# A hybrid layer on one core: k's pairs ahead of q's, constants beside values, staging rows moved, buffers resized

## The chip, the core and the metric

The kernel runs on one core of a Trainium2 chip. TensorE multiplies matrices into PSUM; VectorE, ScalarE and GpSimd work on tiles in SBUF; SyncE (SP) issues the transfers, which sixteen DMA engines carry out. Each engine takes its instructions in the order in which the program holds them, and waits at an instruction until what it needs is there. The metric is the device time of one execution in microseconds; a kernel's time is the median of its runs.

## The reference

One step of a layer over 1088 tokens (1024 of a new stream, 64 of a running one, which also sees 512 cached keys). Cut to what matters here:

```python
xn = _rmsnorm(x, p['norm_mix_w'])
z, xbc, dt_raw, q, k, v, gate_ssm, gate_att = jnp.split(xn @ p['w_in'], ...)
...
q = _partial_rope(_rmsnorm(q.reshape(b, t, 16, 64), p['q_norm_w']), q_pos)
k = _partial_rope(_rmsnorm(k.reshape(b, t, 16, 64), p['k_norm_w']), q_pos)
lam = (jnp.exp(jnp.sum(lambda_q1 * lambda_k1)) - jnp.exp(jnp.sum(lambda_q2 * lambda_k2)) + lambda_init)
o = _diff_attention(q, k_all, v_all, q_pos, k_pos, lam)      # softmax 1 - lam * softmax 2, times v
o = _rmsnorm(o, p['subln_w']) * (1.0 - lambda_init)
mix = sigmoid(gate_ssm) * (y_ssm @ w_branch_ssm) + sigmoid(gate_att) * (o @ w_branch_attn)
x = x + mix @ w_out
x = x + ConvFFN(RMSNorm(x))
```

y_ssm comes from a causal convolution of xbc, a scan over chunks of 64 tokens and a gate of z. k and v are outputs too; q is not.

## The kernel before

All activations lie transposed: 128 channels on the partitions, tokens along the row. A product of float32 is made of three matmuls of rounded parts (hi x hi, lo x hi, hi x lo), so every operand exists as a pair hi and lo: a cast on ScalarE (L355) makes hi, a subtraction on VectorE (L356) makes lo.

The stages stand in this order in the program. **Norm and values.** The input is normed into xn. values(f) (L275) makes a quarter of v from two 512 KB blocks of weights; weights() (L137) loads a block, casts it (L149) and subtracts (L150), with a scheduler's priority `ahead`, which moves these three ahead of other work on their engines. values(0) and values(1) also give dt; steps() (L305) makes the scan's step sizes from it (TensorE L327 to L340). differences() (L367) makes sums of quarters of xn for the next stage, with rows in the pool tt, and stores one of them in t_sc. values(2) and values(3) follow.

**Pairs.** q and k are made by a Strassen-Winograd scheme, two feature blocks at a time: a pair is seven products of blocks, seven() (L563), whose matmuls are L575. Eight pairs run in the order q0, q2, q4, q6, k0, k2, k4, k6. left_blocks() (L426) loads a pair's weights and makes the seven left operands; the next pair's are made during a pair. Each finished row of q or k is squared (L486), and kept raw in r_q or r_k in DRAM (L478).

**finish().** When the four pairs of q (or k) are done, Heads.finish() (L504) sums the squares by four matmuls (L509), makes the reciprocal root (Ln L217, Exp L218, Square L219 on ScalarE) and then runs sixteen rows of 128 channels by 544 tokens: load the raw row (L514), multiply (L516, L518), for k store it as an output (L520), split into hi and lo (L355, L356), store both in q_st or k_st (L524). The tag `fr` of the pool `mid` holds the raw rows, two of them. q's finish runs a row at a time between the products of k's pairs; before it, cached() splits the cached keys in the same manner. k's finish has no pairs left to lie under.

**Filler and attention.** stream() (L689) yields the gate, z and convolution projections in chunks of 24 matmuls (project(), L160; matmuls L156 to L158), each with an evacuation: Tanh for a gate (L641), Tanh (L650) and a multiply (L651) for z. Their rows are staged in the pool st. fill(n) puts n chunks into the program. After k's finish come twelve chunks (FIRST), which the scheduler interleaves with it, then six PSUM banks are released, `mid` is released, `st` is released and made again on the right side of SBUF, and attention runs for eight heads: head_tiles() (L718) loads q, k and v of a head (L722), scores are L764 and L765, and 1.74 chunks of filler go to each unit. Ahead of head 0 stand the constants: wsub (L846), and lam and nlam (L849 to L854). After attention comes the scan with 1.5 chunks for each of its steps, then the branches (attention's o_sc into m_sc and the first half of y_sc into n_sc, as filler under the scan's last steps; the second half of y_sc, whose rows are loaded by L178 and to which g_sc, n_sc and m_sc are brought by L188, after it), the output projection and the FFN.

SP's queue is in order: a store that waits for its row holds all loads behind it.

Of the kernel before, what the change touches and what calls it, by code (L numbers as in the profile page):

```python
# [9 lines left out]
F32 = mybir.dt.float32  # L10
R32 = mybir.dt.float32r
AF = mybir.ActivationFunctionType
ALU = mybir.AluOpType
# [4 lines left out]
P = 128  # L18
# [38 lines left out]
LAST = 200  # L57
ATT_STEPS = 1.74
FIRST = 12
LEFT = dict(fa=8, fs=2)  # L60
MID = dict(fu=4, pr=4, cc=4, ss=4, fr=2)
MIDW = 544
HALF = T // 2
SCAN_STEPS = 1.5
# [17 lines left out]
def hybrid_layer(ctx: ExitStack, tc: tile.TileContext, xT, prm, cst, rope, wvd, win, wbs, wba, wout, wup, wdn,  # L82
# [27 lines left out]
    ident, ones, tri, blk = (con[:, i * P : (i + 1) * P] for i in range(4))  # L110
    eps_t = cp.tile([P, 1], F32, name="eps_t")
    V.memset(eps_t, EPS)

    def col(o):
        return par[:, o : o + 1]
# [16 lines left out]
    xn = [xn_pool.tile([P, KT, T], R32, name=f"xn_{u}") for u in ("hi", "lo")]  # L132
    parts = [[t[:, :, c : c + w] for t in xn] for c, w in WIDE]

    extra, turn, ahead, quick = None, 0, AHEAD_IN, QUICK

    def weights(block, k, m, pool=None):  # L137
        nonlocal turn
        if pool is None:
            turn = (turn + 1) % 3  # L140
        p, b = (pool, 1) if pool is not None else (extra, 1) if extra is not None and turn == 0 else (wp, 2)
        top = WMAX if p is wp else WDT
        w = p.tile([P, top], F32, name="w_f", tag="w_f", bufs=b)
        hi = p.tile([P, top], R32, name="w_hi", tag="w_hi", bufs=b)
        lo = p.tile([P, top], R32, name="w_lo", tag="w_lo", bufs=b)
        w, hi, lo = (t[:, : k * m].rearrange("p (k m) -> p k m", k=k) for t in (w, hi, lo))
        with tc.high_priority(ahead):
            load(out=w, in_=block.rearrange("p (k m) -> p k m", k=k))
            S.copy(hi, w)  # L149
            V.tensor_tensor(out=lo, in0=w, in1=hi, op=ALU.subtract)  # L150
        return hi, lo
# [57 lines left out]
    def run(gen):  # L209
        for _ in gen:  # L210
            pass
# [92 lines left out]
    with tc.tile_pool(name="qk", bufs=1) as qk:  # L304
        def steps():  # L305
            small = lambda n: qk.tile([P, 9, 32], F32, name=n, tag=n)
            da, e, t, t2 = (small(n) for n in ("da", "de", "dt", "dt2"))
            u = dtw
            act(e, u, AF.Abs)
            act(e, e, AF.Exp, scale=-1.0)  # L310
            V.tensor_scalar_add(t, e, 2.0)
            V.reciprocal(t, t)
            V.tensor_tensor(out=t, in0=t, in1=e, op=ALU.mult)
            V.tensor_tensor(out=t2, in0=t, in1=t, op=ALU.mult)
            V.tensor_scalar(e, t2, 1.0 / 17, None, ALU.mult)
            for n in (15, 13, 11, 9, 7, 5, 3):
                V.scalar_tensor_tensor(e, e, 1.0 / n, t2, ALU.add, ALU.mult)
            V.scalar_tensor_tensor(e, e, 1.0, t, ALU.add, ALU.mult)
            V.tensor_scalar_max(u, u, 0.0)
            V.scalar_tensor_tensor(dt_tok, e, 2.0, u, ALU.mult, ALU.add)  # L320
            an = qk.tile([P, 32], F32, name="an")
            act(an, par[:, O_AL : O_AL + 32], AF.Exp)
            V.scalar_tensor_tensor(da, dt_tok, -1.0, an.unsqueeze(1).to_broadcast([P, 9, 32]), ALU.mult, ALU.mult)
            V.memset(da[TS:, 8, :], 0.0)
            flat = lambda x: x.rearrange("p a b -> p (a b)")
            pa = stat(288)
            PE.matmul(pa, tri, flat(da), start=True, stop=True)  # L327
# [4 lines left out]
            V.tensor_tensor(out=flat(dtw), in0=pl, in1=flat(nacum), op=ALU.add)  # L332
            act(dtw, dtw, AF.Exp)
            V.tensor_tensor(out=dtw, in0=dtw, in1=dt_tok, op=ALU.mult)
            af = qk.tile([P, T], F32, name="af")[:32]
            for c, w in WIDE:
                pf = stat(512)
                for i in range(c // P, -(-(c + w) // P)):
                    n = min(P, T - i * P)
                    PE.matmul(pf[:32, i * P - c : i * P - c + n], da[:n, i], tri[:n, :n], start=True, stop=True)  # L340
                V.tensor_copy(af[:, c : c + w], pf[:32, :w])
            load(out=a_sc, in_=af)

        steps()
        load(out=d_sc, in_=dts.rearrange("p a b c -> p (a b c)"))
    dp.release()

# [6 lines left out]
    def split(hi, lo, src):  # L354
        S.copy(hi, src)  # L355
        V.tensor_tensor(out=lo, in0=src, in1=hi, op=ALU.subtract)  # L356
# [47 lines left out]
            differences(s, j)  # L404
    for u in range(2):
        load(out=b_sc[P * u : P * (u + 1), :].rearrange("p (a t) -> p a t", a=4), in_=xn[u][:, :4, HALF:].bitcast(F32))
    for f in (2, 3):
        run(values(f))
    tt.release()
    s1.close()  # L410
    st.release()
    extra.release()
# [13 lines left out]
    def left_blocks(b0, b1):  # L426

        def row(tag, name, dt=F32):
            return lp.tile([P, 512], dt, name=name, tag=tag, bufs=LEFT[tag])

        a = []
        for b in (b0, b1):
            w = wp.tile([P, WMAX], F32, name="w_f", tag="w_f", bufs=2)
            load(out=w, in_=b)
            a += [w[:, :512], w[:, 512:]]
        q11, q12, q21, q22 = a
        s1, s2 = (row("fs", n) for n in ("ws1", "ws2"))
# [11 lines left out]
        G.tensor_tensor(out=q21, in0=q11, in1=q21, op=ALU.subtract)  # L449
        yield own(q21)  # L450
        t = [wp.tile([P, WMAX], R32, name=n, tag=n, bufs=2) for n in ("w_hi", "w_lo")]
        for i, src in enumerate((s1, q22)):
            hi, lo = (x[:, 512 * i : 512 * i + 512] for x in t)
            split(hi, lo, src)
            yield hi, lo
        G.tensor_tensor(out=s2, in0=q12, in1=s2, op=ALU.subtract)
        hi, lo = (wp.tile([P, WMAX], R32, name=n, tag=n, bufs=2)[:, :512] for n in ("w_hi", "w_lo"))
        split(hi, lo, s2)
        yield hi, lo

    psb = ExitStack()
    more = psb.enter_context(tc.tile_pool(name="psb", bufs=6, space=PSUM)), 6
# [149 lines left out]
    heads = {n: Heads(n) for n in "qk"}  # L612
    both = [(p, s) for p in range(7) for s in range(2)]
    begin = [(p, s) for p in (0, 2, 1, 3, 5, 4, 6) for s in range(2)]
    order = [(n, f, f + 1) for n in "qk" for f in range(0, KT, 2)]
    left, finishing = list(blocks_of(*order[0])), cached()
    for n, (kind, f, g) in enumerate(order):
        coming = blocks_of(*order[n + 1]) if n + 1 < len(order) else iter(())
# [8 lines left out]
            if n + 1 == len(order) and (p, s) == (4, 1):  # L627
                fourth(b_sc)
        left = nxt + list(coming)
        if (kind, f) == ("q", 6):  # L630
            finishing = chain(finishing, heads["q"].finish())
    run(finishing)
    lp.release()
    tu.release()
# [69 lines left out]
            spare -= 1  # L704


    run(heads["k"].finish())
    fill(FIRST)
    psb.close()
    more = None, 0  # L710
    mid.release()
    st.release()
    st = tc.alloc_tile_pool(name="st", bufs=1, side="right")
    cv_pool = tc.alloc_tile_pool(name="cv", bufs=1, side="right")

    with (tc.tile_pool(name="ak", bufs=1) as ak, tc.tile_pool(name="at", bufs=1) as at,
          tc.tile_pool(name="psc", bufs=1, space=PSUM) as psc, tc.tile_pool(name="psa", bufs=1, space=PSUM) as pa):
        def head_tiles(h):  # L718
            def fetch(name, n, b, parts):
# [120 lines left out]
                    load(out=o_sc[D * u + P * h : D * u + P * (h + 1), b0 * P : b0 * P + w], in_=t.bitcast(F32))  # L840

        tiles = head_tiles(0)
        lam = at.tile([P, 4], F32, name="lam")
        lt = at.tile([P, 512], F32, name="lt", tag="a_t", bufs=AT)[:, :64]
        wsub = at.tile([P, P], F32, name="wsub")
        V.tensor_scalar_mul(wsub, par[:, O_SUB : O_SUB + P], 1.0 - LAMBDA_INIT)  # L846
        for i in range(2):
            a = O_LAM + 128 * i
            V.tensor_tensor(out=lt, in0=par[:, a : a + 64], in1=par[:, a + 64 : a + 128], op=ALU.mult)  # L849
            V.reduce_sum(lam[:, i : i + 1], lt, axis=AX.X)  # L850
            act(lam[:, i : i + 1], lam[:, i : i + 1], AF.Exp)
        nlam = at.tile([P, 1], F32, name="nlam")
        V.tensor_tensor(out=nlam, in0=lam[:, 1:2], in1=lam[:, 0:1], op=ALU.subtract)
        V.tensor_scalar_add(nlam, nlam, -LAMBDA_INIT)  # L854

        late = []
        for h in range(8):
            if h:
# [18 lines left out]
            late = [lambda h=h, o=o_t, q=ssq, s=s0: head_out(h, o, q, s)]  # L877
        late[0]()


    with (tc.tile_pool(name="sin", bufs=1) as sin, tc.tile_pool(name="sp", bufs=1) as sp,
          tc.tile_pool(name="psi", bufs=1, space=PSUM) as psi, tc.tile_pool(name="pss", bufs=1, space=PSUM) as pss):
# [133 lines left out]

        def branch_tiles():
            nonlocal bs
            cv_pool.release()
            st.release()  # L1020
# [558 lines left out]
```

## Time and profile before

| | us |
|---|---|
| median of 3 runs | 2549.25 (2539.55 to 2556.42) |
| the profiled execution, its own time | 2546.22 |
| its span, first to last instruction | 2544.4 |
| TensorE busy | 2433.2 |
| VectorE busy | 1678.5 |
| ScalarE busy | 1206.7 |
| GpSimd busy | 804.0 |
| granted TensorE clock, mean | 0.984 |

The span is the time between the first and the last instruction in the profile; the execution's own time is a little longer. A row of the list of waits reads: engine, operation and line that waited, the engine, tile and line that released it, the total, the number of times, the longest. A row of the timeline reads: start, duration, engine, line, operation, tile written <- tiles read, shape, and in brackets the idle time of the engine just before it with its releaser.

### The profile page before, as it was taken

To read this page: it belongs to the slowest core of one execution; us is meant where nothing else is said; L and a number is where in the kernel's file an instruction comes from. 1 tells how busy PE (TensorE), PEld (TensorE's weight loads), DVE (VectorE), ACT (ScalarE), POOL (GpSimd) and SP (SyncE) were. 2 spreads that over 40 slices of the span, in tenths; PEclk is the share of its full clock that TensorE was granted. 3 is DMA by queue.
4 is the path that set the end of the run, shared out by engine and by line. 5 is a ranking of instruction groups with operands and counts; after the bars stand their busy time and mean duration, and the time that the engine had idled before them with its cause. 6 is when DMAs were issued, how large, how long until landed. Compare 5 with 4: busy or idle time off the path is not lost. (4 is left out here: it accounts for less than half of the span.)

```text
span 2544.4 us, 45910 instructions
## 1 busy us (share of the span) xinstructions
PE 2433.2 (96%) x17154; PEld 2351.0 (92%) x17154; DVE 1678.5 (66%) x2885; ACT 1206.7 (47%) x2616; POOL 804.0 (32%) x784
## 2 busy tenths in 40 slices
PE   8999985999999999999899999899999999999999
PEld 7999985999999999999798889899999999999999
DVE  7666843775588758645676675564677777777765
ACT  6234442564466646536665564324544343344541
POOL 3235320000011001003443332002466766665445
PEclk9999987999999999999999999999999999999999
DMA  5254789445435543436689763656223444348865
GB/s 176 97 190 171 242 293 307 129 128 166 136 104 152 166 124 112 122 105 206 195 258 304 213 205 116 224 157 214 85 94 126 135 130 137 128 164 247 217 158 169
DMA packets 293776, 432.74 MB, mean 170 GB/s; under 512 B 34576, under 2 KB 210320, under 8 KB 293552
## 3 DMA queue, kind: packets, MB, share of 16 engines
q1 hardware_dynamic: 288944, 420.89, 52.1%
q0 software_dynamic: 4608, 8.91, 2.3%
q8 instruction: 135, 2.21, 0.4%
q14 instruction: 89, 0.73, 0.1%
HBM read 282.18 MB, written 147.52 MB: 169 GB/s over the span
## 5 line engine op out<-in xcount | busy, mean ns | idle before, releaser
L156 PE MATMUL mm<-xn_hi,w_hi 128*128 128x384 f32 (+1 forms) x1632 | 549.3, 337 | 36.7 <-DVE zr L651 26.7
L158 PE MATMUL mm<-xn_hi,w_lo 128*128 128x384 f32 (+1 forms) x1632 | 541.1, 332 | 0.0
L157 PE MATMUL mm<-xn_lo,w_hi 128*128 128x384 f32 (+1 forms) x1632 | 540.9, 331 | 0.0
L156 PEld LDWEIGHTS mm<-xn_hi,w_hi 128*128 128x128 f32 x1632 | 309.4, 190 | 45.9 <-DVE zr L651 27.0
L157 PEld LDWEIGHTS mm<-xn_lo,w_hi 128*128 128x128 f32 x1632 | 309.3, 190 | 5.5 <-issue 3.8
L158 PEld LDWEIGHTS mm<-xn_hi,w_lo 128*128 128x128 f32 x1632 | 308.9, 189 | 1.6 <-issue 1.0
L1270 PE MATMUL mx<-m,w_hi 128*128 128x272 f32 x1068 | 204.2, 289 | 2.6 <-DVE down L1420 2.5
L1270 PE MATMUL mx<-n,wh 128*128 128x272 f32 x1068 | 205.0, 289 | 1.6 <-ACT u L1406 1.0
L150 DVE TENSOR_TENSOR w_lo<-w_f,w_hi 128x1024 fp32r<-128x1024 f32 (+1 forms) x104 | 140.0, 1346 | 63.6 <-ACT w_hi L149 61.5
L1270 PEld LDWEIGHTS mx<-m,w_hi 128*128 128x128 f32 x1068 | 168.6, 189 | 3.2 <-DVE down L1420 3.0
L1270 PEld LDWEIGHTS mx<-n,wh 128*128 128x128 f32 x1068 | 168.1, 189 | 2.0 <-ACT u L1406 1.2
L1270 PE MATMUL mx<-m,w_lo 128*128 128x272 f32 x534 | 154.2, 289 | 0.0
L1270 PE MATMUL mx<-n,wl 128*128 128x272 f32 x534 | 154.1, 289 | 0.0
L149 ACT CAST w_hi<-w_f 128x1024 fp32r<-128x1024 f32 (+1 forms) x104 | 109.0, 1048 | 75.6 <-PE mm L157 49.0
L778 ACT ACTIVATE p_t<-sc,mx 128x1024 f32<-128x1024 f32 (+5 forms) x144 | 106.1, 740 | 80.2 <-DVE mx L769 52.9
L680 DVE SCALAR_TENSOR_TENSOR cc<-pre,par,cc 128x384 f32<-128x384 f32 (+1 forms) x216 | 126.0, 584 | 14.0 <-ACT cc L678 10.1
L668 POOL COPY pre<-pre 128x3 f32<-128x3 f32 x48 | 14.3, 299 | 367.4 <-ACT pre L669 266.1
L920 POOL TENSOR_SCALAR_AFFINE_SELECT bc<-bc 128x1024 f32<-128x1024 f32 (+1 forms) x36 | 43.0, 1196 | 249.6 <-DMA w_f<-in_win_dram 130.0
L1074 ACT CAST w_hi<-ws 128x512 fp32r<-128x512 f32 (+1 forms) x64 | 38.9, 607 | 148.8 <-PE mx L1270 91.8
L1297 POOL TENSOR_TENSOR hb<-hb,cc 128x480 f32<-128x480 f32 (+2 forms) x66 | 92.4, 1413 | 42.1 <-ACT w_hi L1074 21.7
L1270 PEld LDWEIGHTS mx<-m,w_lo 128*128 128x128 f32 x534 | 100.8, 189 | 0.0
L1270 PEld LDWEIGHTS mx<-n,wl 128*128 128x128 f32 x534 | 100.3, 188 | 0.0
(431 smaller groups left out, 6839.7 us busy)
## 6 DMA issues: line engine op xcount, KB each, us to landing
w_f<-in_win_dram SPq DMA_DIRECT2D x76, 512.0 KB, 3.9
w_f<-in_wup_dram SPq DMA_DIRECT2D x44, 512.0 KB, 3.8
hr<-q_sc SPq DMA_DIRECT2D x70, 272.0 KB, 4.7
bc<-a_sc SPq DMA_DIRECT2D x32, 512.0 KB, 5.9
q_sc<-hb SPq DMA_DIRECT2D x44, 272.0 KB, 2.3
gb<-q_sc SPq DMA_DIRECT2D x44, 272.0 KB, 4.0
x_sc<-cc SPq DMA_DIRECT2D x48, 192.0 KB, 2.4
q_sc<-gb SPq DMA_DIRECT2D x33, 272.0 KB, 2.2
```

Of the source, the lines that this page charges most:

```text
L149: S.copy(hi, w)
L150: V.tensor_tensor(out=lo, in0=w, in1=hi, op=ALU.subtract)
L156: PE.matmul(ps, a_hi, b_hi, start=i == 0, stop=False)
L157: PE.matmul(ps, a_hi, b_lo, start=False, stop=False)
L158: PE.matmul(ps, a_lo, b_hi, start=False, stop=i == n - 1)
L668: G.tensor_copy(pre[:, 0:3], tail)
L680: V.scalar_tensor_tensor(cc[:, :m], pre[:, i : i + m], cw(i), cc[:, :m], ALU.mult, ALU.add)
L778: act(p_t[:n, :nk], sc[c][:n, :nk], AF.Exp, bias=mx[:n, c : c + 1], accum_out=dst)
L920: G.affine_select(bc[:L, :, :L], bc[:L, :, :L], [[0, 8], [1, L]], ALU.is_ge, -1e30, base=0, channel_multiplier=-1)
L1074: S.copy(hi, src)
L1270: PE.matmul(ps, w[x][:, c], b[y][:, k], start=start and k == t == 0, stop=k == nk - 1 and t == 2, skip_group_check=not start)
L1297: G.tensor_tensor(out=hb[h][:, o : o + n], in0=hb[h][:, o : o + n], in1=cc[:, d : d + n], op=ALU.mult)
```

## The change

It does five things.

- k's four pairs come first, then q's. So k's finish, with its output stores, runs between the products of q's pairs, and q's finish stands behind the last pair. Three chunks of filler (fill(3)) are put ahead of it. The tag `fr` has four buffers instead of two.
- The constants of attention (wsub, lam, nlam) are made in a tile that stays, right behind steps(), in place of tiles of attention's pool; nothing they need comes from the layer's data.
- The pool of staging rows, st0, made on the left at the end of the pairs, stays through attention; the one on the right is made after attention. The tiles at and ak of attention change places.
- The last two value blocks have `lead = 0`: the loads and casts of their weights get no priority. values(3) takes its second block's weights from a new pool, wx2, which lies over the released pool tt.
- The tag `fa` of the left operands has six buffers instead of eight; q21 moves from there into one half of the weights' buffers.

```diff
-LEFT = dict(fa=8, fs=2)
-MID = dict(fu=4, pr=4, cc=4, ss=4, fr=2)
+LEFT = dict(fa=6, fs=2)
+MID = dict(fu=4, pr=4, cc=4, ss=4, fr=4)
...
+    lam = cp.tile([P, 3], F32, name="lam")
+    nlam, wsub = lam[:, 2:3], par[:, O_SUB : O_SUB + P]
...
-        with tc.high_priority(ahead):
+        with tc.high_priority(ahead if lead is None else lead):
...
         steps()
+        V.tensor_scalar_mul(wsub, wsub, 1.0 - LAMBDA_INIT)
+        for i in range(2):
+            a = O_LAM + 128 * i
+            lt = par[:, a : a + 64]
+            V.tensor_tensor(out=lt, in0=lt, in1=par[:, a + 64 : a + 128], op=ALU.mult)
+            V.reduce_sum(lam[:, i : i + 1], lt, axis=AX.X)
+            act(lam[:, i : i + 1], lam[:, i : i + 1], AF.Exp)
+        V.tensor_tensor(out=nlam, in0=lam[:, 1:2], in1=lam[:, 0:1], op=ALU.subtract)
+        V.tensor_scalar_add(nlam, nlam, -LAMBDA_INIT)
...
-    for f in (2, 3):
-        run(values(f))
+    lead = 0
+    run(values(2))
     tt.release()
+    more_w = tc.alloc_tile_pool(name="wx2", bufs=1)
+    run(values(3, None, (None, more_w)))
+    more_w.release()
+    lead = None
...
-        yield own(q21)
-        t = [wp.tile([P, WMAX], R32, name=n, tag=n, bufs=2) for n in ("w_hi", "w_lo")]
-        for i, src in enumerate((s1, q22)):
...
+        for two in ((q21, s1), (q22, None)):
+            t = [wp.tile([P, WMAX], R32, name=n, tag=n, bufs=2) for n in ("w_hi", "w_lo")]
+            for i, src in enumerate(two):
...
-    order = [(n, f, f + 1) for n in "qk" for f in range(0, KT, 2)]
+    order = [(n, f, f + 1) for n in "kq" for f in range(0, KT, 2)]
...
-        if (kind, f) == ("q", 6):
-            finishing = chain(finishing, heads["q"].finish())
+        if (kind, f) == ("k", 6):
+            finishing = chain(finishing, heads["k"].finish())
...
-    run(heads["k"].finish())
+    fill(3)
+    run(heads["q"].finish())
     fill(FIRST)
     psb.close()
     more = None, 0
     mid.release()
-    st.release()
-    st = tc.alloc_tile_pool(name="st", bufs=1, side="right")
     cv_pool = tc.alloc_tile_pool(name="cv", bufs=1, side="right")
...
         tiles = head_tiles(0)
-        lam = at.tile([P, 4], F32, name="lam")
...
-        V.tensor_scalar_add(nlam, nlam, -LAMBDA_INIT)
...
         late[0]()
 
+    st.release()
+    st = tc.alloc_tile_pool(name="st", bufs=1, side="right")
```

Where the instructions stand, at three places. First ScalarE at the end of the pairs, where the statistics of the last finish are made (mm and mx are PSUM banks, qn the statistics, gt a gate tile's row, qh a finished row's hi part). Before, of k's finish:

```order
L217 ACTIVATE qn<-mm,eps_t 128x272
L218 ACTIVATE qn<-qn 128x272
L217 ACTIVATE qn<-mm,eps_t 128x272
L219 ACTIVATE qn<-qn 128x272
L218 ACTIVATE qn<-qn 128x272
L219 ACTIVATE qn<-qn 128x272
L217 ACTIVATE qn<-mx,eps_t 128x272
L218 ACTIVATE qn<-qn 128x272
L217 ACTIVATE qn<-mx,eps_t 128x272
L219 ACTIVATE qn<-qn 128x272
L218 ACTIVATE qn<-qn 128x272
L219 ACTIVATE qn<-qn 128x272
```

After, of q's finish (its lines L219, L220, L221 are L217, L218, L219 of before, its L655 is L641):

```order
L655 ACTIVATE gt<-mx 128x320
L219 ACT_TABLE_LOAD
L219 ACTIVATE qn<-mx,eps_t 128x272
L220 ACT_TABLE_LOAD
L220 ACTIVATE qn<-qn 128x272
L219 ACT_TABLE_LOAD
L219 ACTIVATE qn<-mx,eps_t 128x272
L221 ACTIVATE qn<-qn 128x272
L220 ACT_TABLE_LOAD
L220 ACTIVATE qn<-qn 128x272
L221 ACTIVATE qn<-qn 128x272
L219 ACT_TABLE_LOAD
```

The first gate tile's Tanh now stands ahead of the statistics, and a table load stands before every change between Ln and Exp.

Second, VectorE at the end of the last finish (raw and ql are a finished row and its lo part, zr a z tile's row, w_lo a weight's lo part). Before, with the constants and two evacuations of z that follow the rows:

```order
L518 SCALAR_TENSOR_TENSOR raw<-raw,par,ss 128x544
L356 TENSOR_TENSOR ql<-raw,qh 128x544
L846 TENSOR_SCALAR wsub<-par 128x128
L849 TENSOR_TENSOR lt<-par 128x64
L863 MEMSET ssq 128x9
L864 MEMSET s_4768 128x9
L863 MEMSET ssq 128x9
L864 MEMSET s_5678 128x9
L850 TENSOR_REDUCE lam<-lt 128x1
L651 SCALAR_TENSOR_TENSOR zr<-zr,mm 128x384
L849 TENSOR_TENSOR lt<-par 128x64
L651 SCALAR_TENSOR_TENSOR zr<-zr,mm 128x384
```

After (L532, L367 and L665 are L518, L356 and L651 of before):

```order
L367 TENSOR_TENSOR ql<-raw,qh 128x544
L532 SCALAR_TENSOR_TENSOR raw<-raw,wq_1861,ss 128x544
L152 TENSOR_TENSOR w_lo<-w_f,w_hi 128x1024
L665 SCALAR_TENSOR_TENSOR zr<-zr,mx 128x320
L367 TENSOR_TENSOR ql<-raw,qh 128x544
L665 SCALAR_TENSOR_TENSOR zr<-zr,mm 128x384
L367 TENSOR_TENSOR ql<-raw,qh 128x544
L665 SCALAR_TENSOR_TENSOR zr<-zr,mm 128x384
L152 TENSOR_TENSOR w_lo<-w_f,w_hi 128x1024
L665 SCALAR_TENSOR_TENSOR zr<-zr,mm 128x320
```

The evacuations of z stand between the last rows and behind them, and the constants are gone from here.

Third, ScalarE at the third and fourth value blocks (t1h and t_... are rows of differences, dts the results of steps(), vo an evacuated value tile, wh and w_hi of width 512 left operands of the first pair). Before:

```order
L355 CAST t_1197<-f_1276 128x544
L355 CAST w_hi<-w_f 128x512
L355 CAST t_1199<-f_1290 128x544
L286 COPY vo<-mm 128x256
L331 ACTIVATE dts<-st 128x288
L286 COPY vo<-mm 128x256
L333 ACTIVATE dts<-dts 128x288
L286 COPY vo<-mx 128x256 x2
L355 CAST wh<-w_f 128x512
L355 CAST w_hi<-ws_1853 128x512
L286 COPY vo<-mx 128x256
```

After (L366, L333, L335, L288 and L151 are L355, L331, L333, L286 and L149 of before):

```order
L366 CAST t_1207<-f_1286 128x544
L366 CAST t_1209<-f_1300 128x544
L333 ACTIVATE dts<-st 128x288
L335 ACTIVATE dts<-dts 128x288
L151 CAST w_hi<-w_f 128x1024
L288 COPY vo<-mm 128x256 x2
L288 COPY vo<-mx 128x256 x3
L288 COPY vo<-mm 128x256 x2
L288 COPY vo<-mx 128x256
L288 COPY vo<-mx 64x256
L366 CAST wh<-w_f 128x512
L366 CAST w_hi<-ws_1867 128x512
```

The cast of the last value block's second weights (w_hi, width 1024), which stood ahead of the rows shown of before, now stands behind the results of steps(), and the first pair's casts stand behind all value tiles.

More of the change, by code (lines that the diff above doesn't have):

```diff
@@ L133, in hybrid_layer @@
     parts = [[t[:, :, c : c + w] for t in xn] for c, w in WIDE]
-    extra, turn, ahead, quick = None, 0, AHEAD_IN, QUICK
+    extra, turn, ahead, quick, lead = None, 0, AHEAD_IN, QUICK, None
     def weights(block, k, m, pool=None):
@@ L449, in left_blocks @@
         G.tensor_tensor(out=q21, in0=q11, in1=q21, op=ALU.subtract)
-        yield own(q21)
-        t = [wp.tile([P, WMAX], R32, name=n, tag=n, bufs=2) for n in ("w_hi", "w_lo")]
-        for i, src in enumerate((s1, q22)):
[L453 to L459, printed above, removed]
+        for two in ((q21, s1), (q22, None)):
+            t = [wp.tile([P, WMAX], R32, name=n, tag=n, bufs=2) for n in ("w_hi", "w_lo")]
+            for i, src in enumerate(two):
+                if src is None:
+                    src = s2
+                    G.tensor_tensor(out=s2, in0=q12, in1=s2, op=ALU.subtract)
+                hi, lo = (x[:, 512 * i : 512 * i + 512] for x in t)
+                split(hi, lo, src)
+                yield hi, lo
     psb = ExitStack()
@@ L711, in hybrid_layer @@
     mid.release()
-    st.release()
-    st = tc.alloc_tile_pool(name="st", bufs=1, side="right")
     cv_pool = tc.alloc_tile_pool(name="cv", bufs=1, side="right")
-    with (tc.tile_pool(name="ak", bufs=1) as ak, tc.tile_pool(name="at", bufs=1) as at,
+    with (tc.tile_pool(name="at", bufs=1) as at, tc.tile_pool(name="ak", bufs=1) as ak,
           tc.tile_pool(name="psc", bufs=1, space=PSUM) as psc, tc.tile_pool(name="psa", bufs=1, space=PSUM) as pa):
@@ L842, in hybrid_layer @@
         tiles = head_tiles(0)
-        lam = at.tile([P, 4], F32, name="lam")
[L844 to L853, printed above, removed]
-        V.tensor_scalar_add(nlam, nlam, -LAMBDA_INIT)
         late = []
@@ L1018, in branch_tiles @@
             nonlocal bs
+            st.release()
             cv_pool.release()
-            st.release()
             bs = tc.alloc_tile_pool(name="bs", bufs=1, side="right")
```

## The prediction

> **What bounds the kernel now.** I read the page first, then the list of waits on TensorE, then the stretches of time around the longest wait, then the instructions in them. On the page TensorE is busy for nearly the whole span; below its line stand six rows of the list of waits (total, times, longest, in us).
>
> ```profile
> PE 2433.2 (96%) x17154; PEld 2351.0 (92%) x17154; DVE 1678.5 (66%) x2885; ACT 1206.7 (47%) x2616; POOL 804.0 (32%) x784
> ...
> PE mm L156 <- DVE zr L651: 26.7, 1, 26.7
> PE mx L575 <- DVE pre L554: 7.4, 2, 5.4
> PE mm L156 <- DVE b_g L199: 7.1, 1, 7.1
> ...
> PE mm L156 <- ACT w_hi L149: 5.1, 1, 5.1
> ...
> PE mm L509 <- POOL ss L487: 4.7, 1, 4.7
> ...
> PE mm L156 <- ACT xn_hi L179: 3.0, 1, 3.0
> ```
>
> TensorE stands for 2544.4 - 2433.2 = 111 us in all, and one wait is a quarter of that: 26.7 us for an evacuation of a z tile. The change adds and removes no matmul, so all it can win is idle time and clock. Where that wait comes from shows in the stretches (us of busy time, counts, granted clock, DMA share, GB/s) and in the rows at its two ends.
>
> ```profile
> 350.00:400.00 50.00, 50.00 (x296) 49.65 (x296) 22.79 (x36) 18.85 (x35) 0.00 (x0) 0.98 0.85 286
> 400.00:450.00 50.00, 22.72 (x122) 21.79 (x121) 17.15 (x35) 9.41 (x17) 0.10 (x1) 0.73 1.02 302
> 353.00:427.00 74.00, 54.69 (x330) 54.37 (x328) 31.30 (x46) 21.41 (x36) 0.00 (x0) 0.89 0.94 310
> ```
>
> ```profile
> 342.64 0.44 DVE L554 TENSOR_TENSOR pre<-mx,u 128x272 f32<-128x272 f32 x1 [2.02 <-PE mx L575]
> 352.39 1.36 DVE L516 TENSOR_TENSOR raw<-raw,ss 128x544 f32<-128x544 f32 x2
> 424.02 0.78 DVE L518 SCALAR_TENSOR_TENSOR raw<-raw,par,ss 128x544 f32<-128x544 f32 x1 [3.48 <-DMA raw<-r_k]
> 433.25 0.23 DVE L846 TENSOR_SCALAR wsub<-par 128x128 f32<-128x128 f32 x1 [6.96 <-DMA cv_t<-in_cv_dram]
> 434.37 0.55 DVE L651 SCALAR_TENSOR_TENSOR zr<-zr,mm 128x384 f32<-128x384 f32 x1
> ```
>
> ```profile
> 433.13 0.87 ACT L650 ACTIVATE zr<-mm 128x384 f32<-128x384 f32 x2 [7.60 <-DMA k_st<-ql]
> ```
>
> ```profile
> 399.17 0.34 PE L156 MATMUL mm<-xn_hi,w_hi 128*128 128x384 f32 x1
> 407.35 0.34 PE L158 MATMUL mm<-xn_hi,w_lo 128*128 128x384 f32 x1
> 434.38 0.63 PE L156 MATMUL mm<-xn_hi,w_hi 128*128 128x320 f32 x1 [26.69 <-DVE zr L651]
> 438.07 0.31 PE L158 MATMUL mm<-xn_hi,w_lo 128*128 128x320 f32 x1
> 439.54 0.34 PE L156 MATMUL mm<-xn_hi,w_hi 128*128 128x384 f32 x1
> 441.45 0.39 PE L764 MATMUL sc<-kh_t,q_t 128*128 128x512 f32 x1
> ```
>
> The last pair's matmuls end at T0 = 342.6. k's sixteen rows run from 352.39 to 424.02, (424.02 - 352.39) / 15 = 4.8 us each, each waiting for its load. DMA is the limit there: share 0.94, 310 GB/s. TensorE, with both remaining banks full, waits at 407.7. Its evacuation is held twice: ScalarE's L650 waits for the last k_st store, because the staging tile lies over the rows' memory, and VectorE's L651 stands behind wsub (L846), which waits for memory that other loads release.
>
> **The end of the pairs, part by part.** After the change it is q's finish that stands there; k's rows lie under q's pairs. A q row has one transfer fewer, since q has no plain output. The sizes come from the DMA issues between 345 and 435 us (count, KB each, us to landing), the end of the stores from the rows of k_st.
>
> ```profile
> out_dram<-raw SPq DMA_DIRECT2D x16, 272.0 KB, 2.9
> k_st<-qh SPq DMA_DIRECT2D x16, 272.0 KB, 3.7
> ```
>
> ```profile
> L524 SPq DMA_DIRECT2D k_st<-ql x10: 319/518/1354, 384.0 to 427.5; - x10
> ```
>
> Of a k row the load, the kT store and two k_st stores are 4 x 272 KB = 1.11 MB, sixteen 17.8 MB. From 353 to 427, 74 us x 310 GB/s = 22.9 MB moved, so the rest (the filler's weights and stores) took 5.1 MB in 54.7 us of busy TensorE, 93 KB per us. q's sixteen rows move 3 x 272 KB each, 13.4 MB. With TensorE fed, 310 - 93 = 217 KB per us is left: 62 us. Starting at T0+12 (before: 352.39 - 342.64 = 9.8, and the statistics now come after two chunks of filler), the last store issues at about T0+74. Head 0's loads follow on SP; before, the last store issued at 427.5 and the first scores began at 441.45, 14 us later, so now at T0+88.
>
> TensorE's own work to that point: a chunk of 24 matmuls takes (407.35 + 0.17 - 399.17) / 2 = 4.2 us at 384 columns and, at (439.54 - 438.07) / 10 = 0.147 us each, 3.5 us at 320; two of the former to one of the latter mean 3.96. Nineteen chunks now stand ahead of the first scores, where fifteen and a half stood: 19 x 3.96 = 75, with the statistics and a wait of about 1 for them 77.4. So some 88 - 77.4 = 10.6 us of idle are left, at the banks (the z evacuations stand between the last rows on VectorE) or at the scores. Before it was 4.7 (L509) + 26.7 = 31.4. **Term: -20.8.** Bounds: nothing but a wait of 2 if rows go at VectorE's and ScalarE's own pace, and all of 31 if they go at k's 4.8 us (both below as rivals).
>
> The four row buffers for two: half of a row's 4.8 us could be the wait for a buffer whose kT store has to land (2.9 us). With DMA at 0.94 I count nothing for it beyond the byte sum; that there is slack in it is the first rival.
>
> The first fourteen matmuls after the wait took 438.07 - 434.38 = 3.7 us instead of 14 x 0.147 = 2.1: 1.6 us of lower clock, lost again only if the new waits are long. **-1.0** (0 to -1.6).
>
> TensorE's 5.4 us in a pair at L575 fall in the last pairs, where VectorE's L554 and ScalarE stand behind the row work of q's finish. Now k's rows stand there, with a kT store more each, so nothing is sure: **-2.4** (0 to -5.4).
>
> **ScalarE's tables.** Before, q's and k's statistics (Ln L217, Exp L218, L219) ran ahead of the first Tanh, with no load of a table. Now fill(3) puts Tanh first and eight table loads lie in the statistics. What a load costs shows at another norm, with the statistics before for comparison.
>
> ```profile
> 348.66 0.49 ACT L217 ACTIVATE qn<-mm,eps_t 128x272 f32<-128x272 f32 x1 [3.45 <-PE mm L509]
> ...
> 353.61 0.43 ACT L219 ACTIVATE qn<-qn 128x272 f32<-128x272 f32 x1
> ...
> 1588.10 1.28 ACT L217 ACT_TABLE_LOAD   x1
> 1589.40 0.56 ACT L217 ACTIVATE gn<-grs,eps_t 128x320 f32<-128x320 f32 x1
> 1589.98 1.28 ACT L218 ACT_TABLE_LOAD   x1
> 1591.28 0.47 ACT L218 ACTIVATE gn<-gn 128x320 f32<-128x320 f32 x1
> ```
>
> The chain was 353.61 + 0.43 - 348.66 = 5.4 us and becomes 5.4 + 8 x 1.3 = 16 us, to about T0+28. It needs the first half of that (T0+20) for rows 1 to 8; the loads of the first four rows and the filler use the DMA meanwhile, so the byte sum stands and the term is 0, at most 8 if DMA is idle until T0+20. The Trainium skill (ScalarE: Activation LUTs, What ACT_TABLE_LOAD costs) gives about 2.66 us for every switch, 1.28 of it the load and the rest a drain; the trace has the 1.28 but the next ACTIVATE starts 1.30 us after the load, so the row decides; by the page the eight would be 21 us. The same page (Table sets) says that one set holds ln and exp, so that ln, exp costs one load; here L218 loads again right after L217, so no such saving is counted.
>
> **Values and the first pair.** The third and fourth value blocks no longer prefetch weights (lead = 0), and the second half of block three takes its weights' buffer from memory that the differences' rows hold until their last stores. The rows: the last prefetched cast, the statistics of dt, the last work on them, and what a 512 KB load takes (6: count, KB, us to landing); then the casts for pair 0.
>
> ```profile
> 122.63 1.04 ACT L149 CAST w_hi<-w_f 128x1024 fp32r<-128x1024 f32 x1
> 136.43 0.44 ACT L333 ACTIVATE dts<-dts 128x288 f32<-128x288 f32 x1 [1.73 <-DVE dts L332]
> 142.10 0.62 ACT L355 CAST wh<-w_f 128x512 fp32r<-128x512 f32 x1 [3.01 <-DMA a_sc<-af]
> 147.00 0.62 ACT L355 CAST wh<-w_f 128x512 fp32r<-128x512 f32 x1 [0.56 <-POOL w_f L449]
> ```
>
> ```profile
> 130.59 0.65 PE L327 MATMUL st<-da,con 128*128 128x288 f32 x2
> ```
>
> ```profile
> w_f<-in_win_dram SPq DMA_DIRECT2D x76, 512.0 KB, 3.9
> ```
>
> Before, TensorE waits 5.1 us for the cast at 122.63 and then goes through. After, it does the first halves at once, stands until the statistics at 130.59 (about 5 us), and then again until the late weights are there: load at about 132, 3.9 us, cast after L333 at 136.43 + 0.44 = 136.9 and 1.04 long. With 3.5 us of statistics between, that is 5 us less some overlap. **+3.5** (0 to +7). Pair 0's casts, at 142 to 147 ahead of its matmuls, now come after the last evacuation of values, since their rows lie over that buffer: about three casts of 0.62 and the subtractions behind them, **+2** (0 to +5).
>
> **The small edits.** nlam and wsub move to the kernel's start, seven tiny VectorE and two ScalarE instructions under the first norm: +0.5 (0 to +1). Two row buffers fewer for the left blocks, with their operands in the weights' buffers: 0 (0 to +2), since SP loads a pair ahead.
>
> **The scan's end.** After the first scores all filler is 2.83 chunks ahead, 2.83 x 3.96 = 11.2 us less to do when the scan ends.
>
> ```profile
> 1595.42 0.37 SPq L974 DMA_DIRECT2D y_sc<-y  x1
> ...
> 1606.17 1.37 SPq L178 DMA_DIRECT2D b_f<-y_sc  x3
> ```
>
> ```profile
> 1610.06 0.62 PE L156 MATMUL mm<-xn_hi,w_hi 128*128 128x384 f32 x2 [2.98 <-ACT xn_hi L179]
> ```
>
> Before, TensorE worked until 1610.06 - 2.98 = 1607.1 and waited 3.0. Now it runs dry at 1607.1 - 11.2 = 1595.9. The b_f loads, which stood behind n_sc stores, can issue when y_sc has landed, about 1599; with 1610.06 - 1606.17 = 3.9 us to the first matmul that is 1603, a wait of 7. **+4.0** (0 to +11). The 7.1 us for b_g come afterwards and stay.
>
> **The sum:** -20.8 - 1.0 - 2.4 + 3.5 + 2.0 + 0.5 + 4.0 = -14.2 us. The profiled execution took 2546.2 us, so 2532; it lies 3 us under the median of 2549.25, so 2535 on the median's footing.
>
> **The rivals.** *Rows at the engines' pace.* A row needs 0.78 us of VectorE at L518, a cast and a subtraction; with four buffers and no kT store to wait for, loads run ahead. If 217 KB per us is too low by a quarter, the last store is at T0+61 and scores can start at T0+75, before TensorE is there. Idle falls to about 2 (-29.4), clock -1.6, L575 -5.4, and half the costs (+5): -31, 2518. For it: the page's peaks; against: share 1.02 from 400 to 450.
>
> *Rows at k's pace (slower).* If the table loads hold the first row to T0+22 and each row takes the 4.8 us of before, for DMA latency rather than bytes, the sixteenth is at T0+22+72 = T0+94 and scores at T0+108: idle 31, no gain, and +10 of costs less 2.4: +8, 2557. The wait is then at the first scores, not at the banks. It decides from idle 25, a last store at T0+88. For it: every row of before waited for its load; against: a quarter fewer bytes.
>
> *The page's drain.* If each switch holds ScalarE for twice the 1.3 us of the rows, the rows start some 10 us later and the byte sum shifts with them: 2545. The rows at 1588 to 1591 speak against it. That price is the one that the Trainium skill (ScalarE: Activation LUTs, What ACT_TABLE_LOAD costs) states.
>
> *The wait does not go.* The new order still has the z evacuations between rows on VectorE; this lies within the forecast's idle of 10.6.
>
> **The numbers.** What a measurement of this kernel tells from no change is about 1%, 25 us: below 2524 is faster, above 2575 slower. Forecast 0.43, its own range 2522 to 2550; engines' pace 0.30, 2508 to 2525; k's pace 0.18, 2550 to 2580, for which values and the scan's end at their upper bounds (+18 for +7.5) go over 2575; the drain 0.04; 0.05 for what I have not seen. Faster: 0.28 of the engines' pace and 0.05 of the forecast, 0.33. Slower: 0.07 of k's pace, 0.03 of the rest, 0.10. Same 0.57. The range leaves out the outer parts of the two rivals: 2508 to 2564.
>
> **What would show it.** A wait at L156 or at L764 of together 5 to 16 us between T0 and the first scores; k's rows without a wait of TensorE at L575 over 3 us; eight loads of 1.28 us on ScalarE between T0 and T0+30 with no gap behind them; two waits of TensorE in values of some 5 us; a wait for xn_hi of 5 to 9 us after the scan. It is wrong if q's rows run at 4.5 us or more each, or at 3 or less, or if TensorE stands elsewhere in the pairs, for weights that SP now issues behind k's kT stores.

## The result, and the profile after

The changed kernel takes 2531.81 us (median of 5 runs, 2527.99 to 2536.89); its ratio to the kernel before is 0.9934, interval 0.9906 to 0.9962. Run again word for word beside the second group of experiments it took 2535.3 us, ratio 0.9959 (0.9943 to 0.9975). So it is faster by half a per cent, 10 to 17 us, where 14 were forecast. The profiled execution has a span of 2530.0 us, 14.4 less than before.

First the page's line of TensorE and the list of its waits after (total, times, longest, in us). L158, L201, L181, L589, L568, L566, L329, L777 and L665 are L156, L199, L179, L575, L554, L552, L327, L764 and L651 of before.

```profile
PE 2438.8 (96%) x17154; PEld 2355.6 (93%) x17154; DVE 1684.4 (67%) x2885; ACT 1214.9 (48%) x2624; POOL 798.7 (32%) x784
...
PE mm L158 <- ACT xn_hi L181: 6.8, 1, 6.8
...
PE mm L158 <- DVE b_g L201: 5.1, 1, 5.1
PE mx L589 <- DVE pre L568: 4.9, 3, 2.2
PE mm L158 <- ACT pre L566: 4.3, 1, 4.3
PE st L329 <- DVE da L326: 4.2, 1, 4.2
...
PE sc L777 <- DMA kh_t<-k_st: 3.9, 1, 3.9
...
PE mm L158 <- issue: 2.5, 1, 2.5
...
PE mm L158 <- DVE zr L665: 1.8, 2, 1.2
```

The wait of 26.7 us is gone: 1.8 at the banks and 3.9 at the scores are left. The first scores start no earlier for that (441.94 against 441.45); what is gained is that TensorE has done about 20 chunks of filler by then instead of 15.5. TensorE stands for 2530.0 - 2438.8 = 91 us instead of 111, so 20 us of idle went, but its busy time grew by 5.6 us with the same matmuls: they ran slower somewhere. The stretches show where (busy us of the engines, then clock, DMA share, GB/s).

```profile
130.00:135.00 5.00, 5.00 (x22) 3.54 (x21) 4.90 (x8) 1.54 (x3) 1.56 (x1) 0.55 0.16 57
135.00:140.00 5.00, 2.53 (x17) 2.11 (x15) 2.96 (x5) 1.49 (x2) 0.00 (x0) 0.79 0.70 251
140.00:145.00 5.00, 5.00 (x25) 5.00 (x26) 0.00 (x0) 0.49 (x2) 0.00 (x0) 0.53 0.09 30
370.00:427.00 57.00, 54.71 (x328) 53.81 (x328) 35.20 (x55) 31.13 (x51) 0.00 (x0) 1.00 0.75 268
```

In values the granted clock is 0.53 to 0.55 behind each of the two waits (da, and the late weights, which stand in the list as issue). And while q's rows run, 370 to 427, DMA has a share of 0.75 and 268 GB/s, less than the 310 of before: bytes do not limit them. What the work on the rows waits for (us, times), first before, between 350 and 430, then after, between 370 and 440:

```profile
  DMA raw<-r_k: 28.4, 8
```

```profile
  DMA q_st<-qh: 16.6, 9
  DMA q_st<-ql: 9.8, 6
...
  DMA raw<-r_q: 0.2, 1
```

With two row buffers the rows wait for their loads. With four they wait until the halves qh and ql of earlier rows are stored; these halves share the four buffers of another tag, cc. The next rows are the first pair's first matmul, the first scores, the two ends of the statistics on ScalarE, and the row work on VectorE.

```profile
161.24 0.39 PE L589 MATMUL mx<-xn_hi,wh 128*128 128x272 f32 x1 [1.02 <-ACT wh L366]
...
441.94 0.77 PE L777 MATMUL sc<-kh_t,q_t 128*128 128x512 f32 x1 [3.95 <-DMA kh_t<-k_st]
```

```profile
366.48 1.28 ACT L219 ACT_TABLE_LOAD   x1
367.77 0.49 ACT L219 ACTIVATE qn<-mx,eps_t 128x272 f32<-128x272 f32 x1
...
382.01 0.42 ACT L221 ACTIVATE qn<-qn 128x272 f32<-128x272 f32 x1
```

```profile
L532 DVE SCALAR_TENSOR_TENSOR raw<-raw,wq,ss x12: 774/777/784, 376.7 to 422.0; 128x544 f32<-128x544 f32 x12
...
L530 DVE TENSOR_TENSOR raw<-raw,ss x4: 716/719/724, 375.4 to 402.6; 128x544 f32<-128x544 f32 x4
```

Pair 0 starts at 161.2, where it started at 152.7 before: 8.5 us were lost ahead of it. The last pair's matmuls end at 357.7. The sixteen rows run from 375.4 to 422.0, 46.6 / 15 = 3.1 us each, and the statistics take 382.4 - 366.5 = 15.9 us with the eight table loads.

### The profile page after: what moved, and what is told of

It reads as the page before. It is cut to its first block, busy times and chain, and to the rows that moved or that the text cites. A ratio compares the mean times of both kernels' runs of the same rounds, so it can differ in the third digit from the quotient of the medians.

```text
span 2530.0 us, 45915 instructions
## 1 busy us (share of the span) xinstructions
PE 2438.8 (96%) x17154; PEld 2355.6 (93%) x17154; DVE 1684.4 (67%) x2885; ACT 1214.9 (48%) x2624; POOL 798.7 (32%) x784
## 4 chain that ended last, share of the span: by engine, by line
PE 72%; DMA 9%; DVE 9%; ACT 4%; issue 3%; POOL 1%; SPq 1%; DVEq 0%; ACTq 0%; POOLq 0%
PE mx L1272 15%; PE mm L158 10%; PE mm L160 10%; PE mm L159 10%; PE mm L1272 6%; PE po L825 3%; PE mx L589 2%; PE mx L158 2%; PE mx L159 2%; PE mx L160 2%; PE sc L778 2%; PE sc L777 1%; PE pt L806 1%; DMA hr<-q_sc 1%; PE yi L933 1%
## 5 line engine op out<-in xcount | busy, mean ns | idle before, releaser
L158 PE MATMUL mm<-xn_hi,w_hi 128*128 128x384 f32 (+1 forms) x1648 | 550.9, 334 | 22.1 <-ACT xn_hi L181 6.8
L158 PEld LDWEIGHTS mm<-xn_hi,w_hi 128*128 128x128 f32 x1648 | 312.9, 190 | 27.5 <-ACT xn_hi L181 7.1
L152 DVE TENSOR_TENSOR w_lo<-w_f,w_hi 128x1024 fp32r<-128x1024 f32 (+1 forms) x104 | 131.3, 1264 | 69.8 <-ACT w_hi L151 69.6
L151 ACT CAST w_hi<-w_f 128x1024 fp32r<-128x1024 f32 (+1 forms) x104 | 108.9, 1047 | 82.6 <-PE mm L159 55.4
L1077 DVE TENSOR_TENSOR wl<-w_f,wh 128x512 fp32r<-128x512 f32 (+1 forms) x96 | 87.4, 911 | 22.6 <-ACT wh L1076 21.9
```

Source lines behind the costliest of these rows:

```text
L158: PE.matmul(ps, a_hi, b_hi, start=i == 0, stop=False)
```

## The experiments

Twelve more measurements followed, in three groups, each beside runs of the kernel before (2545 to 2548 us there); each ratio is to those, with its interval. Kernels of different groups are best compared by their ratios. First single parts of the change were undone.

**Values as before.**

```diff
-    lead = 0
-    run(values(2))
-    tt.release()
-    more_w = tc.alloc_tile_pool(name="wx2", bufs=1)
-    run(values(3, None, (None, more_w)))
-    more_w.release()
-    lead = None
+    for f in (2, 3):
+        run(values(f))
+    tt.release()
```

> The changed kernel with the value blocks as before: their weights are loaded ahead again and the last block takes no buffer over the differences' rows. Theory (late weights and the lower clock that follows cost 8 us): values end at 152 to 154 us instead of 160.3, the clock between 125 and 145 is 0.9 or more, and the time is 7 to 9 us under the changed kernel's 2531.8, 2524 (ratio to before 0.990). Rival (TensorE stands there for the sums of dt in any case and the clock falls for that): 1 to 3 us less, 2530.

2529.51 us, 0.9929 (0.9914 to 0.9944). The two stretches of low clock between 130 and 145 are gone; left is a shorter one behind the wait of 5.2 us for w_hi, as the kernel before has it (0.83 between 125 and 130, before 0.78). Pair 0 starts 7.7 us earlier; the rows are of the kernel with values as before.

```profile
130.00:135.00 5.00, 4.53 (x32) 3.63 (x30) 4.95 (x6) 2.20 (x5) 2.38 (x3) 1.00 0.38 133
135.00:140.00 5.00, 5.00 (x41) 4.71 (x42) 4.95 (x6) 3.75 (x9) 4.12 (x3) 1.00 0.33 123
140.00:145.00 5.00, 5.00 (x44) 5.00 (x43) 3.50 (x5) 0.87 (x3) 2.07 (x1) 1.00 0.49 109
...
153.53 0.36 PE L585 MATMUL mx<-xn_hi,wh 128*128 128x272 f32 x1 [0.55 <-issue]
```

So the place and the price there are shown. The time is not the 2524 of the theory; it is near the rival's 2530, though the clock did not stay low, as the rival had it. Of the 7.7 us, 5.7 are still there when the scan ends (TensorE goes on at 1593.83 instead of 1599.49), the profiled execution keeps 1.3 at its end, and the medians keep 2 to 6, depending on which of the two measurements of the changed kernel is taken. Where the rest went was not followed.

**q's pairs first again**, with all else of the change.

```diff
-    order = [(n, f, f + 1) for n in "kq" ...]
+    order = [(n, f, f + 1) for n in "qk" ...]
...
-    run(heads["q"].finish())
+    run(heads["k"].finish())
```

> The changed kernel with q's pairs first again, so k's finish with its 16 output stores stands behind the last pair; all else stays. Theory (bytes: 17.8 MB of rows at 217 KB per us are 82 us instead of 62): TensorE stands some 20 us longer between the last pair and the first scores than in the changed kernel, 2549 to 2553, ratio 1.000. Rival (the long wait of before came from the staging rows over the row buffers and from wsub in front of the evacuations, and both are gone here too): 4 to 6 us longer, 2537, ratio 0.995.

2533.87 us, 0.9943 (0.9928 to 0.9959): no slower than the changed kernel. The byte theory is off by 15 us. k's rows, four transfers each, run from 361.8 to 416.1 at (416.1 - 361.8) / 15 = 3.6 us:

```profile
L532 DVE SCALAR_TENSOR_TENSOR raw<-raw,par,ss x12: 777/782/786, 363.1 to 416.1; 128x544 f32<-128x544 f32 x12
...
L530 DVE TENSOR_TENSOR raw<-raw,ss x4: 718/722/726, 361.8 to 394.8; 128x544 f32<-128x544 f32 x4
```

**The staging pool made again on the right**, over the row buffers; k's pairs first.

```diff
     mid.release()
+    st.release()
+    st = tc.alloc_tile_pool(name="st", bufs=1, side="right")
     cv_pool = tc.alloc_tile_pool(name="cv", bufs=1, side="right")
...
```

The tiles at and ak change back as well.

> The changed kernel with the staging pool made again on the right, over the row buffers, ahead of attention, as before; k's pairs first. Theory (the order of the pairs does most, the staging a little): the first evacuations into the new pool wait for the landing of q's last stores at about 431 us, where TensorE with two banks left would stand 3 to 6 us, 2536, ratio 0.995. Rival (the staging was the main cause): 15 us or more, 2547, ratio 0.999.

2542.58 us, 0.9981 (0.9969 to 0.9993): 7 to 11 us slower than the changed kernel, between the theory and the rival; half of the gain or more is gone. A wait at the banks is back (8.7 us at the longest), and ScalarE's evacuation waits for the last row's store; first TensorE's row, then ScalarE's between 395 and 445 us:

```profile
PE mm L158 <- DVE zr L665: 9.7, 2, 8.7
```

```profile
ACT zr L664 <- DMA q_st<-ql: 5.8, 1, 5.8
```

**fill(3) behind the finish.**

```diff
-    fill(3)
     run(heads["q"].finish())
-    fill(FIRST)
+    fill(FIRST + 3)
```

> The changed kernel with fill(3) behind q's finish instead of ahead (fifteen chunks there in all), so no Tanh stands ahead of the statistics and the eight table loads are gone. Theory (the table loads lie beside DMA and filler, off the path): TensorE waits some 4.7 us for the sums of squares again, and rows that start 10 us earlier take the 6 us of waits at the scores away: within 3 us of the changed kernel, 2529 to 2535. Rival (the table loads hold the rows, and the rows set the end): 6 us or more faster, 2525.

2534.18 us, 0.995 (0.9935 to 0.9965): as the theory has it, no change. The table loads of the finish are gone and the last store issues at 411.0 instead of 427.8, first the row of this kernel, then that of the changed one, and it buys nothing: a wait of 5.2 us for the sums of squares is back, and L568 holds TensorE for 11.1 us in all instead of 4.9 (6.2 of it in the last pair, where the changed kernel stands 4.3 us at L566).

```profile
L538 SPq DMA_DIRECT2D q_st<-ql x16: 319/406/1108, 368.1 to 411.0; - x16
```

```profile
L538 SPq DMA_DIRECT2D q_st<-ql x16: 319/414/1159, 384.9 to 427.8; - x16
```

In the second group the changed kernel ran again, with one more undoing, and two parts were put alone into the kernel before.

> The changed kernel once more, word for word, beside the kernels of this group: 2528 to 2534, ratio to before 0.991 to 0.996. It is the base for the comparisons of a few microseconds.

2535.3 us, 0.9959 (0.9943 to 0.9975), 1 us above the expected range.

**Two row buffers** in the changed kernel (`fr=2` for `fr=4`).

> The changed kernel with two row buffers instead of four. Theory of the prediction (bytes set the rows' pace, 217 KB per us beside the filler): rows stay near 3.1 us each, within 3 us of the changed kernel, ratio 0.993 to 0.995. Rival (the pace is set by the time that a buffer takes through load, multiply and stores, so by the number of buffers): rows of q take 4.2 us or more, the last store comes 12 to 16 us later, and the time is 8 to 14 us longer, 2542, ratio 0.998.

2554.66 us, 1.0029 (1.0012 to 1.0046): 19 us slower than the changed kernel beside it and slower than before. With two buffers k's rows do not keep up with q's pairs, and two waits show it: for the quarter of xn that is loaded again at the end of the pairs, on an SP queue that still issues k's rows there, and at the banks; below them stands q's row work.

```profile
PE mx L158 <- DMA xn_hi<-b_sc: 10.0, 1, 10.0
PE mm L158 <- DVE zr L665: 9.2, 3, 4.6
```

```profile
L532 DVE SCALAR_TENSOR_TENSOR raw<-raw,wq,ss x12: 778/784/786, 391.6 to 446.7; 128x544 f32<-128x544 f32 x12
L530 DVE TENSOR_TENSOR raw<-raw,ss x2: 719/722/726, 417.7 to 419.5; 128x544 f32<-128x544 f32 x2
```

The last fourteen of q's rows need (446.7 - 391.6) / 13 = 4.2 us each. The work on them waits for the loads raw<-r_q again, 30.0 us in nine waits. The number of buffers sets the pace, as the rival said, and the cost is larger than it said.

**Four row buffers alone** in the kernel before (with the six left operands that make room).

```diff
-LEFT = dict(fa=8, fs=2)
-MID = dict(fu=4, pr=4, cc=4, ss=4, fr=2)
+LEFT = dict(fa=6, fs=2)
+MID = dict(fu=4, pr=4, cc=4, ss=4, fr=4)
```

> The kernel before with four row buffers for two, and the six left operands and the weights' halves of q21 that make room for them; nothing else of the change. Bytes theory: k's rows already move at 310 GB/s, so the wait of 26.7 us shrinks by 3 us at most, 2546, ratio 0.999. Buffer theory: rows go at 3.6 us as in the kernel with q's pairs first, the last store comes at about 412 instead of 427.5, the wait shrinks by 10 to 16 us, 2536, ratio 0.995.

2528.13 us, 0.9933 (0.9918 to 0.9948). This edit alone does at least as much as the whole change. First the wait that is left, then the stretch of the rows:

```profile
PE mm L156 <- DVE zr L650: 12.2, 1, 12.2
```

```profile
347.00:407.00 60.00, 55.58 (x334) 55.26 (x332) 31.80 (x47) 21.93 (x38) 0.00 (x0) 0.98 0.97 349
```

The rows of k move at 349 GB/s; the 310 of before, at a share of 0.94, was no ceiling. They take 3.4 us each (347.2 to 398.7), and the wait shrank by 14.5 us, as the buffer theory had it; the time is 8 us better than its 2536.

**The staging rows left in place, with the constants early, alone** in the kernel before (at and ak change places here too).

> The kernel before with the staging rows left where they are through attention and the constants made beside values; two row buffers, q's pairs first. Staging theory (the evacuations stood behind the last row's stores and behind wsub): the evacuations go between the rows, the wait at the banks falls to 10 us or less, and what is left is at the scores; 10 to 14 us faster, 2536, ratio 0.995. Rival (rows at 4.8 us end at 427 in any case, so the wait only moves to the scores): 0 to 4 us faster, ratio 0.999.

2521.45 us, 0.9911 (0.9895 to 0.9926): 25 us faster, more than the staging theory hoped for. The waits of TensorE between the last pair and the first scores, then the stretch of the rows:

```profile
PE mm L520 <- POOL ss L498: 4.6, 1, 4.6
PE sc L773 <- DMA kh_t<-k_st: 2.5, 1, 2.5
```

```profile
352.00:420.00 68.00, 68.00 (x412) 67.94 (x412) 35.00 (x52) 25.31 (x43) 0.00 (x0) 1.00 0.93 322
```

With q first, k's finish last and two row buffers, TensorE never stands under the rows. The first scores start at 434.82, and again about 20 chunks of filler are done by then.

The third group split this and put the parts together. **The constants alone:**

> The kernel before with the constants made beside values; the staging pool is still made again over the row buffers. Theory (the evacuation on ScalarE waits for the last row's stores, since its tile lies over the rows' memory; wsub only stands in line behind the same event): the wait at the banks stays at 25 us or more, 0 to 2 us faster, ratio 0.999 to 1.000. Rival (wsub in front of the evacuations on VectorE held them): 7 us or more faster, ratio 0.997 or less.

2547.53 us, 1.0002 (0.9989 to 1.0016), and the wait is still there. So the constants alone give nothing, and the gain of the kernel above needs the staging pool. Whether the pool alone, with wsub still in front of the evacuations, gives all of it was not run.

```profile
PE mm L158 <- DVE zr L662: 26.1, 1, 26.1
```

**Staging left, constants early and four row buffers**, the rest as before:

> The kernel before with the staging rows left, the constants beside values, and four row buffers: the two edits that each took the wait down, together. If they work on one wait, the sum is not 18 + 25 us: rows of k at 3.4 us take the remaining 2.5 us at the scores away, 2517 to 2521, ratio 0.989 to 0.991. If the rows' pace costs elsewhere too (more filler moved ahead of the scores), 2522 to 2526.

2511.79 us, 0.9869 (0.9851 to 0.9888): 33 us faster than before, more than either part, 17 to 23 us faster than the changed kernel by the ratios, and faster than expected. Between the last pair and the scores TensorE waits only for the sums of squares and 1.1 us for kl_t.

```profile
PE mm L519 <- POOL ss L497: 5.1, 1, 5.1
PE sc L773 <- DMA kl_t<-k_st: 1.1, 1, 1.1
```

**The changed kernel with values as before and fill(3) behind the finish.** Its expectation calls the order the only difference to the last kernel; that was wrong, since it also has fifteen chunks ahead of the scores instead of twelve.

> The changed kernel with value blocks as before and without fill(3): against the kernel with staging rows left and four row buffers it differs in the order of k's and q's pairs alone. Theory (the order is worth nothing once rows are not the limit): within 3 us of that kernel. Bytes theory of the prediction (one transfer fewer in each of the last sixteen rows): 6 us or more faster than it.

2526.47 us, 0.9924 (0.9906 to 0.9942): 15 us slower than the last kernel, not faster. In its pairs TensorE waits longer at L564 (the first row; the second is of the last kernel), 6.5 us of it in the last pair, and its wait at the scan's end is 6.6 us where the last kernel has 3.5.

```profile
PE mx L585 <- DVE pre L564: 10.9, 4, 6.5
```

```profile
PE mx L585 <- DVE pre L564: 4.4, 3, 1.7
```

**Less filler under attention**, in the kernel with staging left and four buffers (`ATT_STEPS = 1.70` for 1.74).

> The kernel before with the staging rows left, the constants beside values and four row buffers, and 1.70 chunks of filler for each unit of attention instead of 1.74, so 2.9 chunks (11 us) move from attention to the scan and its end. Theory (the filler that runs dry at the scan's end costs what the prediction put at 4 us): 2 to 5 us faster than the same kernel with 1.74. Rival (the waits at the scan's end stand whatever the filler, or attention opens up as much): 0 to 2 us either way.

2515.01 us, 0.9884 (0.9865 to 0.9903), 3 us slower than with 1.74, within the two intervals: no gain, and the two waits at the scan's end stand as they were (3.4 and 5.2 here, 3.5 and 5.2 without it): the rival.

## Why the prediction came out right, and where its reasons did not

The number was right: forecast 2535, own range 2522 to 2550, measured 2531.8 and 2535.3. That it came so near is luck in good part: the largest term had about the right size for a wrong reason, and errors of several other terms cancelled.

- **The end of the pairs** (-20.8). Idle was forecast to fall from 31.4 to 10.6 us; 3.9 + 1.8 + 0.5 for one late weight = 6.2 are left, so 25.2 went. The step that failed is the byte sum, "DMA is the limit there: share 0.94, 310 GB/s" and "217 KB per us is left: 62 us". With four buffers k's rows move at 349 GB/s, and in the changed kernel q's rows leave DMA at 0.75. Its result came out all the same, since two errors cancelled: counted from the end of the last pair, at 357.7, the rows began at 18 us instead of 12, behind the statistics, and then took 3.1 us each instead of 62 / 16 = 3.9. So the last store issued at 70 us (forecast 74) and the scores began at 84 (forecast 88). The fewer transfers of q were worth nothing that shows: with q first the same kernel takes as long. What took the wait away is the pool of staging rows that no longer lies over the row buffers (25 us, together with the early constants, which alone give nothing) and the four buffers (18 alone). The prediction read that ScalarE's evacuation was held by the last k_st store and gave this no term of its own.
- **Four buffers**, costed at nothing: 18 us in the kernel before, 19 in the changed one. Its clue was in the rows before: each waited for its load, and SP held four of these loads (L514) for the store out_dram<-raw that had to leave the buffer first. The rows of before are done two at a time, 2 x 4.8 = 9.6 us for the round of a buffer. With four, the rows wait for the stores of their halves (the rows above), so the four buffers of cc come next; no run changed those. The first rival had this mechanism (rows at 3.1 us), but its price of -31 us did not come, since other terms took it.
- **ScalarE's tables**, term 0: right. The chain is 15.9 us long, as worked out, the next ACTIVATE starts 1.29 us after a load, and taking the loads away gains nothing. The Trainium skill (ScalarE: Activation LUTs, What ACT_TABLE_LOAD costs) states about 2.66 us for a switch, a drain included; the drain does not show behind any of the eight.
- **Values and the first pair**, +5.5: 8.5 us at pair 0's start. Both waits came (4.2 for the sums, 2.5 for the late weights), each shorter than the 5 of the forecast; the term was mis-sized since it left out the clock, at 0.53 to 0.55 for some 10 us behind two waits, where before one wait cost a shorter stretch (0.78 between 125 and 130). Undone, 7.7 us come back there, but only a part at the end.
- **L575 in the pairs**, -2.4: no gain. The 5.4 us at one place became 4.9 in three and 4.3 at L566, in the last pair again. The order brings that one: with four row buffers the last pair's wait is 3.9 to 6.5 us where k's pairs come first and 1.6 or less where q's do; with two and q first it is 5.1 to 5.4.
- **The scan's end**, a wait of 7 forecast, +4.0: 6.8 measured for xn_hi, 3.0 before; the second one shrank from 7.1 to 5.1. In the kernels with twelve chunks ahead of the scores that first wait is 3.0 to 3.9, in those with fifteen 6.6 to 7.0, so it goes with the three chunks of fill(3). With twelve, less filler under attention does not take it below 3.4, as the run with 1.70 showed.
- **The constants**, +0.5: 1.0002, nothing.
- **The clock behind the long wait**, -1.0: the wait is gone, but chunk 1 runs slow behind the new 4.3 us at L566.

What is left open: the changed kernel is 17 to 23 us slower than the one with staging and buffers alone. Values, k's pairs first and the three chunks lie between them. Each has a price at its place: values 8 us, the order some 4 us in the last pair, the three chunks some 3 us at the scan's end. Undoing values or the order, or moving the chunks behind the finish, gave at most a few microseconds in the whole time, and no run takes the three chunks out of the changed kernel; so that the prices add up to the difference is not shown. Which of the two edits of values is needed for its cost was not run.

## What to carry to other kernels

Before a transfer rate is taken as the limit, ask how many buffers are in flight: here a loop of load, compute and store with two buffers ran at the time of one round trip per buffer (9.6 us for two rows), and DMA's busy share looked full all the same (0.94). When an evacuation waits for a transfer that it does not use, look for the pool whose memory it was given: moving that pool, with the constants made early, was worth more than the five edits together. And a bundle that gains is worth taking apart, since here two of its parts gave twice what the whole did.

## What the runs showed of the hardware

DMA's busy share says little about bytes: 0.94 went with 310 GB/s, 0.97 with 349 on the same kind of rows. A short wait cost TensorE as much clock as a long one here. In the changed kernel the granted clock is 0.50 behind waits of 2.5, 3.9, 4.2 and 4.3 us, for 3 to 6 us each time; behind the 4.3 us at L566 the matmuls of chunk 1 take 0.52 us instead of 0.34 for five microseconds (the rows below, of the changed kernel); behind the 26.7 us of before they were slow for 3.4, from 434.38 to 437.74.

```profile
347.65 0.69 PE L158 MATMUL mm<-xn_hi,w_hi 128*128 128x384 f32 x1 [4.28 <-ACT pre L566]
348.13 0.52 PE L159 MATMUL mm<-xn_lo,w_hi 128*128 128x384 f32 x1
...
352.93 0.34 PE L159 MATMUL mm<-xn_lo,w_hi 128*128 128x384 f32 x1
```
